# Buffer counts in a hybrid encoder layer: a second query buffer, a third raw weight buffer, and g_final in the output ring

## The chip, the cores and the metric

The kernel runs on one core of one Trainium2 chip. The metric is device time in microseconds (us) of one execution, given as the median of several runs. One execution was also taken by the hardware profiler; the rows of the profile come from that one.

## The reference

One step of one encoder layer over 2048 prompt tokens and 32 sample tokens, all in float32, width 1024:

```python
a = rmsnorm(h, g_attn)
qa, ka, va, qb, kb, vb = split_proj(a, w_in)       # one projection, 1024 -> 3072 columns
oa = diff_attn(qa, ka, va)   # 4 heads, two score maps of 64 dims each, 128-dim values:
                             # softmax(map 0) - lam * softmax(map 1), T5 bias, chunk-causal mask
ob = band_attn(qb, kb, vb)   # 8 heads of 64, each 64-token chunk sees itself and 8 before it
h = h + concat(rmsnorm(oa, subln_g) * (1 - lam_init), rmsnorm(ob, out_norm_b)) @ w_out
c = rmsnorm(h, g_mlp)
h = h + square(relu(c @ w_up)) @ w_down            # 1024 -> 4096 -> 1024
h = h + sigmoid(h @ w_ple_gate) * (p @ w_ple_proj)
y = rmsnorm(h, g_final)
```

The new keys and values are outputs too. The sample tokens also attend to a cache of 128 older positions.

## The kernel before, in words

Every float32 operand of a matmul is split into a high and a low part, and each product is made of three matmuls (`mm3`, lines 168 to 170): high by high, high by low, low by high. For a weight this is done by `wunit` (line 155): a DMA of 512 KB into a raw tile `wr` (two buffers), a copy to `wh` on ACT (line 149) and a subtraction to `wl` on POOL (line 153), three buffers each. Only after the subtraction is the raw buffer free for the next load. Every DMA of the kernel is issued by SyncE (line 144), whose queue works in order: a DMA that waits for its buffer holds up all behind it.

Tokens come in four blocks: three of 512, and a last one of 544 with the sample tokens. Half 0 is blocks 0 and 1, half 1 blocks 2 and 3. Written order: projection of half 0, first part of the differential attention (pairs of 128-query tiles 0 to 3, pool `a0`), the rest of the projections with the band attention, second part of the differential attention (pairs 4 to 7 and the sample tokens, pool `a1`), output projection and MLP of half 0 (one block after the other), gate and final norm of block 1, output projection of half 1, gate and final norm of block 0, MLP of half 1 (both blocks together), and the gates and final norms of blocks 2 and 3.

That is the order in which the program is written. The order in which each engine's queue runs is drawn up when the program is built, by a planner: it simulates the engines, prefers what is written earlier, and issues what is ready and has a buffer. So the second part of the attention runs in between the MLP of half 0. Within one ring of buffers, tiles are handed out in written order.

In the differential attention, `attn_a` goes over groups of pairs and, within a group, over 4 heads; for each head it loads the bias `ba` and the keys `ka` (one buffer each), and calls `attn_a_pair` for each pair. That one calls `load_q`, which issues four DMAs of 128 KB for the queries of the pair. The query tile `q` has two buffers in the first part (where `self.small` is true) and one in the second. For each of the pair's two query tiles follow the score matmuls (line 545), a maximum on DVE and the exponential on ACT (line 559), the combination of both maps (line 582); then for every four key tiles a load of values `v`, transposes (line 617) and the matmuls with the values (lines 631 to 633). The groups of the second part are `JA1 = [(4, 5), (6, 7, 8)]`, where 8 stands for the sample tokens: 8 loads of keys and 20 of queries.

The gate (`gate`) and the final norm (`final`) take their tiles from a ring: 8 slots (`uq`) for block 1, 16 slots (`up`) for the others; the same rings hold the MLP's hidden activations `uh` and `ul`. `final` transposes h back, takes the sum of squares and multiplies by 1/rms and by g_final (line 1054). g_final lies in a tile of its own, copied to all 128 partitions by `gfin` (line 962): once for block 1, and once more for the other three after the pools were changed.

Of the kernel before, what the change touches and what calls it, by code (L numbers as in the profile page):

```python
# [12 lines left out]
F32 = mybir.dt.float32  # L13
F32R = mybir.dt.float32r
# [5 lines left out]
P = 128  # L20
D = 1024
# [12 lines left out]
BLK = 544  # L34
# [10 lines left out]
def toks(b):  # L45
    out = []
    for i in range(4):
        out.append((i * P, P))
    if b == 3:
        out.append((512, SS))  # L50
    return out
# [81 lines left out]
class Kern:  # L133
# [20 lines left out]

    def wunit(self, src, shape, hi_eng="act", lo_eng="pool"):
        nc = self.nc
        raw = self.wp.tile([P] + shape, F32, tag="wr", bufs=2, name="wr")
        self.dma(raw, src)
        hi = self.wp.tile([P] + shape, F32R, tag="wh", bufs=3, name="wh")
        lo = self.wp.tile([P] + shape, F32R, tag="wl", bufs=3, name="wl")  # L160
        self.split(hi, lo, raw, hi_eng, lo_eng)
        return hi, lo
# [314 lines left out]

    def load_q(self, pool, gi, t0, n, maps):
        nc = self.nc
        q = pool.tile([P, len(maps), 2, 256], F32R, tag="q", bufs=2 if self.small else 1, name="q")  # L480
        for d in range(2):
            for i, m in enumerate(maps):
                self.dma(
                    q[64 * d : 64 * d + 64, i, :, :n],
                    self.qS[gi, :, 64 * m : 64 * m + 64, t0 : t0 + n].rearrange("l r c -> r l c"),
                )
        return q
# [471 lines left out]
            prev = us  # L959
        self.mlp_down(ch, nf, blocks, prev, st, wk, md)  # L960

    def gfin(self, pool):
        self.gf = pool.tile([P, D], F32, name="gf")
        self.dma(self.gf, self.a["g_final"].unsqueeze(0).broadcast_to([P, D]))

    def gate(self, b, h, up, act, md):
        nc, a = self.nc, self.a
        n, t0 = BN[b], 512 * b
# [48 lines left out]
    def final(self, b, h, up, fk, mm, md=None):  # L1017
        nc, a = self.nc, self.a
        t0 = 512 * b
        sts, yns = {}, {}  # L1020
        phased = md is not None

        def side(c0, tn, q):
            if phased:
                sts[c0] = st_all[:, c0 // P]
            elif q == 0:
                sts[c0] = fk.tile([P, 2], F32, tag="fst", bufs=6, name="fst")
            st = sts[c0]
            yp = (md if phased and q == 1 else mm).tile([P, 512], F32, tag="mm", name="yp")
            for k in range(4):  # L1030
                nc.tensor.transpose(yp[:tn, P * k : P * k + P], h[:, 4 * q + k, c0 : c0 + tn], self.ident)
            if phased and q == 1:
                yns[c0, q] = yp
            else:
                yns[c0, q] = up.tile([P, BLK], F32, tag="u", name="yn")[:, :512]
                nc.vector.tensor_copy(yns[c0, q][:tn], yp[:tn])
            junk = up.tile([P, BLK], F32, tag="u", name="junk")[:tn, :512]
            nc.scalar.activation(junk, yp[:tn], AF.Square, accum_out=st[:tn, q : q + 1])

        if phased:  # L1040
            st_all = fk.tile([P, 5, 2], F32, tag="fsa", name="fsa")
            nc.gpsimd.memset(st_all, 1.0)
            for c0, tn in toks(b):
                side(c0, tn, 0)
                yield
        def emit(c0, tn, r):
            tt = t0 + c0
            dst = a["y_prompt"][0, tt : tt + tn] if tt < SP else a["y_sample"][0, tt - SP : tt - SP + tn]
            for q in range(2):
                src = yn = yns[c0, q]  # L1050
                if phased and q == 1:
                    yn = up.tile([P, BLK], F32, tag="u", name="yo")[:, :512]
                g = self.gf[:tn, 512 * q : 512 * q + 512]
                nc.vector.scalar_tensor_tensor(yn[:tn], src[:tn], r, g, op0=ALU.mult, op1=ALU.mult)
                self.dma(dst[:, 512 * q : 512 * q + 512], yn[:tn])

        if phased:
            for c0, tn in toks(b):
                side(c0, tn, 1)
            ss = fk.tile([P, 5], F32, tag="fss", name="fss")  # L1060
            nc.vector.tensor_tensor(ss, st_all[:, :, 0], st_all[:, :, 1], op=ALU.add)
            r = self.rsqrt(fk, ss, 5, 1.0 / D, EPS, nc.vector, "rfa")
            for i, (c0, tn) in enumerate(toks(b)):
                emit(c0, tn, r[:tn, i : i + 1])
            return
        for c0, tn in toks(b):
            side(c0, tn, 0)
            side(c0, tn, 1)
            st = sts[c0]
            nc.vector.tensor_tensor(st[:tn, 0:1], st[:tn, 0:1], st[:tn, 1:2], op=ALU.add)  # L1070
            emit(c0, tn, self.rsqrt(fk, st[:tn, 0:1], 1, 1.0 / D, EPS, nc.vector, "rf", tn, 5))
            yield

    def run(self):
        tc, nc, a = self.tc, self.nc, self.a
        with ExitStack() as top:

            def opened(stack, name, bufs, space=None, side="left"):
                kw = {} if space is None else {"space": space}
                return stack.enter_context(  # L1080
                    tc.tile_pool(name=name, bufs=bufs, side=side, reuse_waits="tile", **kw)
                )
# [31 lines left out]
            with ExitStack() as x:  # L1114
                pool = opened(x, "a0", 1, side="right")
# [42 lines left out]
            with ExitStack() as x:  # L1158
                pool = opened(x, "a1", 1, side="right")
# [1 line left out]
                    self.attn_a(js, pool, ps_s, ps_t, ps_o)  # L1161
            wk = opened(sq_, "wk", 1)
            fk = opened(sq_, "fk", 1)
            self.gfin(fk)
            acc, cn, st = {}, {}, {}
            def norms(b, act, ps):
                self.colnorm(acc[b][0], b, 1.0 / D, wk, ps, "mm", self.rS)
# [10 lines left out]
            up = Sized(opened(top, "uh", 16, side="right"), BLK)  # L1178
# [24 lines left out]
            psx.close()  # L1203
            wk = opened(top, "wk4", 1)
            fk = opened(top, "fk4", 1)
            self.gfin(fk)
            md = opened(top, "md", 8 - MM, PSUM, "right")
            act = Sized(opened(top, "acth", 4), BLK, True)
            hh = opened(top, "hh", 2, side="right")
# [1 line left out]
            g = self.outproj(3, wk, oa[3], md, acc[3])  # L1211
# [4 lines left out]
            g = self.gate(0, h, up, act, md)  # L1216
# [12 lines left out]
            g = self.gate(3, st[3][0], up, act, md)  # L1229
# [54 lines left out]
```

## Time and profile before

| | us |
|---|---|
| median of 3 runs | 3329.38 |
| lowest and highest | 3328.49, 3332.86 |
| the profiled execution | 3334.02 |
| its span in the profile | 3332.1 |

How to read the profile: PE is TensorE's matmuls, PEld its weight loads, which overlap them, DVE is VectorE, POOL is GpSimd, SPq the queue of SyncE. A row of a group of instructions gives line, engine, operation, written tile and read tiles, the count, the busy time, and the idle time just before them with what ended it. A row of the waits gives who waited for whom, the total in us, how often, and the longest. A row in order of time gives the start, the duration, the instruction, and in brackets the idle time before it. A row of a stretch gives its bounds and length, the busy time and the count of instructions of PE, PEld, DVE, ACT and POOL, then PE's granted clock (1.00 is full), the busy share of the DMA engines and GB/s.

### The profile page before, as it was taken

What the parts mean: (1) busy time and instruction counts of PE and PEld (TensorE: products, weight loads), DVE (VectorE), ACT (ScalarE), POOL (GpSimd) and SP (SyncE); (2) the same over time, 40 slices, a digit from 0 to 9 for tenths busy, and PEclk for the clock granted to TensorE, in tenths of its full rate; (3) what the DMA queues carried; (4) which work ended last, traced back from release to release, by engine and by line L of the source; (5) the groups of instructions that cost most, each with busy time, mean ns of one, the idle gap of its engine ahead of it and who ended that gap; (6) DMA issues with size and microseconds to landing.
All of it is one profiled execution on the core that took longest, in us unless ns stands there. A gap on an engine that the chain in (4) does not pass through costs nothing.

```text
span 3332.1 us, 50114 instructions
## 1 busy us (share of the span) xinstructions
PE 3111.6 (93%) x17881; PEld 2723.4 (82%) x17881; DVE 1674.4 (50%) x3952; ACT 1705.5 (51%) x3717; POOL 1467.9 (44%) x1083
## 2 busy tenths in 40 slices
PE   6988989999999999989899999988989999999998
PEld 6877778889877888778787878877779999999987
DVE  5117777454555544566656665746542322223235
ACT  4226666566665666666666665654443223222245
POOL 4335654432324433534544443555753333333365
PEclk9998899999999999999999999999999999999999
DMA  7488777786788554544644454346631111111133
GB/s 227 160 253 235 214 212 202 213 241 205 209 238 234 159 139 126 143 137 133 197 134 123 129 136 130 121 135 222 181 114 51 45 45 45 45 47 49 45 91 102
DMA packets 519074, 488.93 MB, mean 147 GB/s; under 512 B 37885, under 2 KB 414017, under 8 KB 518825
## 3 DMA queue, kind: packets, MB, share of 16 engines
q1 hardware_dynamic: 518824, 485.73, 50.2%
q8 instruction: 142, 2.33, 0.3%
q14 instruction: 108, 0.88, 0.1%
HBM read 379.06 MB, written 110.49 MB: 147 GB/s over the span
## 4 chain that ended last, share of the span: by engine, by line
PE 71%; DMA 12%; DVE 7%; ACT 3%; issue 3%; POOL 2%; SPq 2%; DVEq 0%; POOLq 0%; ACTq 0%
PE dps L168 6%; PE dps L169 6%; PE dps L170 6%; PE ups L168 6%; PE ups L169 6%; PE ups L170 6%; PE s L545 3%; DMA q<-qS 3%; PE qps L168 3%; PE qps L169 3%; PE qps L170 3%; PE ob L744 2%; PE sb L704 2%; SPq L144 2%; DMA ka<-kS 2%
## 5 line engine op out<-in xcount | busy, mean ns | idle before, releaser
L153 POOL TENSOR_TENSOR wl<-wr,wh 128x1024 fp32r<-128x1024 f32 x338 | 819.8, 2427 | 1027.5 <-ACT wh L149 985.3
L949 DVE TENSOR_TENSOR h<-h,dps 128x512 f32<-128x512 f32 (+1 forms) x640 | 373.1, 585 | 590.9 <-PE dps L170 578.4
L149 ACT ACTIVATE wh<-wr 128x1024 fp32r<-128x1024 f32 x338 | 357.4, 1058 | 539.9 <-PE dps L169 294.8
L168 PE MATMUL dps<-uh,wh 128*128 128x512 f32 (+1 forms) x1280 | 460.6, 360 | 14.8 <-DVE h L949 11.1
L168 PE MATMUL ups<-cH,wh 128*128 128x512 f32 (+1 forms) x1280 | 452.5, 354 | 9.3 <-ACT relu L914 7.7
L170 PE MATMUL dps<-uh,wl 128*128 128x512 f32 (+1 forms) x1280 | 453.0, 355 | 0.0
L169 PE MATMUL dps<-ul,wh 128*128 128x512 f32 (+1 forms) x1280 | 453.0, 354 | 0.0
L170 PE MATMUL ups<-cH,wl 128*128 128x512 f32 (+1 forms) x1280 | 451.9, 353 | 0.0
L169 PE MATMUL ups<-cL,wh 128*128 128x512 f32 (+1 forms) x1280 | 451.9, 353 | 0.0
L168 PEld LDWEIGHTS dps<-uh,wh 128*128 128x128 f32 x1280 | 243.8, 190 | 49.8 <-DVE h L949 16.9
L168 PEld LDWEIGHTS ups<-cH,wh 128*128 128x128 f32 x1280 | 242.2, 189 | 41.3 <-ACT relu L914 7.9
L170 PEld LDWEIGHTS dps<-uh,wl 128*128 128x128 f32 x1280 | 242.9, 190 | 33.4
L169 PEld LDWEIGHTS ups<-cL,wh 128*128 128x128 f32 x1280 | 242.7, 190 | 31.1
L153 POOL TENSOR_TENSOR ul<-relu,uh 128x272 fp32r<-128x272 f32 (+1 forms) x160 | 176.0, 1100 | 206.3 <-ACT uh L149 203.6
L170 PEld LDWEIGHTS ups<-cH,wl 128*128 128x128 f32 x1280 | 242.3, 189 | 30.1
L169 PEld LDWEIGHTS dps<-ul,wh 128*128 128x128 f32 x1280 | 243.2, 190 | 27.0
L545 PE MATMUL s<-ka,q 128*128 128x256 f32 (+4 forms) x784 | 197.2, 357 | 50.4 <-DMA q<-qS 29.1
L168 PE MATMUL qps<-aH,wh 128*128 128x512 f32 (+1 forms) x640 | 230.2, 360 | 6.6 <-ACT wh L149 2.2
L169 PE MATMUL qps<-aL,wh 128*128 128x512 f32 (+1 forms) x640 | 228.3, 357 | 0.0
L170 PE MATMUL qps<-aH,wl 128*128 128x512 f32 (+1 forms) x640 | 227.9, 356 | 0.0
L559 ACT ACTIVATE e<-s,nm 128x512 f32<-128x512 f32 (+3 forms) x256 | 155.2, 611 | 102.7 <-DVE nm L551 65.2
L545 PEld LDWEIGHTS s<-ka,q 128*128 128x128 f32 (+1 forms) x784 | 137.4, 200 | 78.5 <-issue 27.3
(217 smaller groups left out, 7076.9 us busy)
## 6 DMA issues: line engine op xcount, KB each, us to landing
wr<-w_up SPq DMA_DIRECT2D x96, 512.0 KB, 4.2
wr<-w_down SPq DMA_DIRECT2D x96, 512.0 KB, 3.7
wr<-w_in SPq DMA_DIRECT2D x74, 512.0 KB, 4.9
q<-qS SPq DMA_DIRECT2D x256, 128.0 KB, 4.7
v<-vSa SPq DMA_DIRECT2D x64, 512.0 KB, 3.8
ka<-kS SPq DMA_DIRECT2D x32, 512.0 KB, 7.2
wr<-w_out SPq DMA_DIRECT2D x32, 512.0 KB, 5.0
wr<-w_ple_gate SPq DMA_DIRECT2D x32, 512.0 KB, 4.4
```

The source lines that it names most:

```text
L144: self.nc.sync.dma_start(dst, src)
L149: nc.scalar.activation(hi, raw, AF.Copy)
L153: eng.tensor_tensor(lo, raw, hi.bitcast(F32), op=ALU.subtract)
L168: nc.tensor.matmul(ps, lh, rh, start=start and i == 0, stop=False)
L169: nc.tensor.matmul(ps, lh, rl, start=False, stop=False)
L170: nc.tensor.matmul(ps, ll, rh, start=False, stop=stop and i == n - 1)
L545: nc.tensor.matmul(s, q[:, m, hl, P * qi : P * qi + nr], kt[:, m, k0 : k0 + n], start=hl == 0, stop=hl == 1)
L559: nc.scalar.activation(dst, src, AF.Exp, bias=nmx, accum_out=z[:nr, m, bi : bi + 1])
L704: nc.tensor.matmul(s, q[:, 0, hl, P * qi : P * qi + nr], kt[:, c : c + w], start=hl == 0, stop=hl == 1)
L744: nc.tensor.matmul(o[:, qa:qb], vt, pt[:kn, i - kfirst, qa:qb], start=x == 0 and y == 0, stop=x == len(order) - 1 and y == 1,)
L949: nc.vector.tensor_tensor(hv, hv, ps, op=ALU.add)
```

## The change

The raw weight tile gets three buffers. The query tile gets two in both parts of the attention. `gfin` and its resident tile go; `final` loads g_final itself, as two tiles of 512 columns from the ring it is given, at its start, and keeps them to its end.

```diff
     def wunit(self, src, shape, hi_eng="act", lo_eng="pool"):
         nc = self.nc
-        raw = self.wp.tile([P] + shape, F32, tag="wr", bufs=2, name="wr")
+        raw = self.wp.tile([P] + shape, F32, tag="wr", bufs=3, name="wr")
...
     def load_q(self, pool, gi, t0, n, maps):
         nc = self.nc
-        q = pool.tile([P, len(maps), 2, 256], F32R, tag="q", bufs=2 if self.small else 1, name="q")
+        q = pool.tile([P, len(maps), 2, 256], F32R, tag="q", bufs=2, name="q")
...
-    def gfin(self, pool):
-        self.gf = pool.tile([P, D], F32, name="gf")
-        self.dma(self.gf, self.a["g_final"].unsqueeze(0).broadcast_to([P, D]))
-
...
         sts, yns = {}, {}
         phased = md is not None
+        gf = []
+        for q in range(2):
+            gf.append(up.tile([P, BLK], F32, tag="u", name="gf")[:, :512])
+            self.dma(gf[q], a["g_final"][512 * q : 512 * q + 512].unsqueeze(0).broadcast_to([P, 512]))
...
-                g = self.gf[:tn, 512 * q : 512 * q + 512]
+                g = gf[q][:tn]
...
             fk = opened(sq_, "fk", 1)
-            self.gfin(fk)
...
             fk = opened(top, "fk4", 1)
-            self.gfin(fk)
```

## The prediction

> **What bounds the kernel now.** I read the profile page first, then busy time by stage, then the waits of PE in each stage, then the instructions around single stalls in order of time.
>
> ```profile
> span 3332.1 us, 50114 instructions
> PE 3111.6 (93%) x17881; PEld 2723.4 (82%) x17881; DVE 1674.4 (50%) x3952; ACT 1705.5 (51%) x3717; POOL 1467.9 (44%) x1083
> L545 PE MATMUL s<-ka,q 128*128 128x256 f32 (+4 forms) x784 | 197.2, 357 | 50.4 <-DMA q<-qS 29.1
> ```
>
> PE is busy 93% of the span; no other engine passes half, PE's own weight loads apart. So the change pays only where PE stands still, or where its clock is lowered. The score matmuls of the differential attention (line 545) wait 50.4 us, most of it for the query load. Three stretches by stage:
>
> ```profile
> 1350.00:2210.00 860.00, 804.98 (x4017) 672.85 (x4017) 540.16 (x1132) 525.29 (x1205) 396.05 (x283) 0.97 0.49 137
> 2210.00:2500.00 290.00, 255.35 (x1344) 217.67 (x1343) 152.14 (x200) 133.84 (x250) 178.81 (x109) 0.94 0.55 174
> 2500.00:3200.00 700.00, 700.00 (x4330) 634.89 (x4329) 204.32 (x384) 199.47 (x338) 240.84 (x157) 1.00 0.16 48
> ```
>
> The first is the second part of the differential attention, run between the MLP of the first token half: PE is idle 860 − 805 = 55 us. The second is the passage to the second half (gate, output norm, output projection): 35 us idle. The third, the MLP of the second half, has no idle time and full clock; more buffers can give nothing there. The waits of PE in the first:
>
> ```profile
> PE s L545 <- DMA q<-qS: 27.3, 11, 4.1
> PE dps L168 <- DVE h L949: 11.1, 11, 2.0
> PE s L545 <- issue: 4.1, 1, 4.1
> ```
>
> Half of the 55 us are waits for queries. The 4.1 us under "issue" are one more such stall at a head's first pair, just after its four query DMAs, so I count 27.3 + 4.1 = 31.4 us.
>
> **Second query buffer.** With one buffer the load of the next pair starts when the last score matmul of this pair has read the old one. Inside a head this is the whole story (SyncE's issues, then PE, in order of time):
>
> ```profile
> 1476.60 2.54 SPq L144 DMA_DIRECT2D q<-qS  x4
> 1482.84 1.31 PE L545 MATMUL s<-ka,q 128*128 128x384 f32 x6 [2.16 <-DMA q<-qS]
> 1665.57 0.59 PE L545 MATMUL s<-ka,q 128*128 128x384 f32 x2 [1.21 <-DMA q<-qS]
> 1761.85 1.19 PE L545 MATMUL s<-ka,q 128*128 128x512 f32 x2 [2.96 <-DMA q<-qS]
> 1999.80 0.76 PE L545 MATMUL s<-ka,q 128*128 128x512 f32 x2 [3.62 <-DMA q<-qS]
> ```
>
> Four DMAs go out in 2.54 us, the queries are there some six microseconds after the buffer came free, and PE stood 2.16 us. These four stalls inside heads are 2.16 + 1.21 + 2.96 + 3.62 = 9.95 us. A second buffer lets the load go a whole pair earlier (20 pairs in 850 us, so some 40 us), and they go. The other 21.4 us are at a head's first pair:
>
> ```profile
> 1704.82 2.61 SPq L144 DMA_DIRECT2D ka<-kS  x4
> 1708.90 4.37 SPq L144 DMA_DIRECT2D q<-qS  x4
> 1720.93 1.22 PE L545 MATMUL s<-ka,q 128*128 128x512 f32 x2 [4.07 <-DMA q<-qS]
> ```
>
> Here the keys, which keep their one buffer, are loaded too, and the queries queue behind them. With two buffers the queries can go ahead of the keys; the keys are then late next. How much is left I take from the first part of the same attention, which has two query buffers, one key buffer and as many key loads already (4 heads x 2 groups of pairs). Its waits of PE on line 545, from 230 to 600 us:
>
> ```profile
> PE s L545 <- issue: 5.5, 2, 3.2
> PE s L545 <- DMA ka<-kS: 5.2, 3, 2.8
> PE s L545 <- DMA q<-qS: 1.8, 1, 1.8
> ```
>
> That is 12.5 us for 8 key loads. Its keys took 6.8 us from issue to landing in the median, those of the second part 7.5 us:
>
> ```profile
> DMA to landing us min/median/max: 3.6/6.8/8.2
> DMA to landing us min/median/max: 5.2/7.5/12.0
> ```
>
> So 12.5 x 7.5 / 6.8 = 13.8 us should remain, and 31.4 − 13.8 = **17.6 us** go. Bounds: 9.95 (only the stalls inside heads) to 31.4 us (all). I take the value of the first part because it is the same code with the same two buffers.
>
> **The clock after a stall.** The column before the last two is the granted clock:
>
> ```profile
> 1450.00:1460.00 10.00, 9.72 (x46) 8.30 (x47) 6.11 (x12) 2.69 (x7) 0.00 (x0) 0.83 0.36 120
> 1480.00:1490.00 10.00, 7.31 (x37) 5.80 (x37) 7.19 (x11) 5.44 (x12) 6.91 (x6) 1.00 0.32 87
> 1530.00:1540.00 10.00, 9.19 (x35) 7.69 (x36) 3.04 (x5) 1.73 (x3) 2.40 (x1) 0.70 0.27 93
> 1760.00:1770.00 10.00, 8.15 (x35) 6.83 (x36) 8.19 (x14) 5.56 (x11) 2.58 (x2) 0.83 0.27 74
> 2070.00:2080.00 10.00, 7.84 (x38) 6.88 (x39) 2.98 (x8) 2.51 (x5) 0.00 (x0) 0.83 0.87 241
> ```
>
> After the stall of 2.16 us (1482.84) the clock stayed full; after the one of 2.96 us (1761.85) ten microseconds ran at 0.83, a loss of 1.7 us. Of the query stalls six are followed by a window at 0.83 (the first and last are shown) and one by 0.70: 6 x 1.7 + 3.0 = 13.2 us. I let it fall with the stalls, 17.6 / 31.4 = 0.56 of it: **7.4 us**. Bounds: 3.4 (the two windows after stalls inside heads) to 13.2 us. [...]
>
> **Third raw weight buffer.** Every weight unit is a 512 KB load, a copy to high parts on ACT and a subtraction on POOL that frees the raw buffer. From 2210 to 2500 us PE waits for weights:
>
> ```profile
> PE gps L168 <- ACT wh L149: 7.4, 1, 7.4
> PE ops L168 <- ACT wh L149: 3.7, 2, 3.0
> PE ops L170 <- POOL wl L153: 1.2, 2, 0.9
> 2381.75 8.22 SPq L144 DMA_DIRECT2D tmp<-hS  x4
> 2390.57 0.38 SPq L144 DMA_DIRECT2D wr<-w_ple_gate  x1
> 2397.44 0.80 PE L168 MATMUL gps<-hH,wh 128*128 128x512 f32 x1 [7.44 <-ACT wh L149]
> 2390.00:2400.00 10.00, 2.56 (x6) 2.10 (x7) 10.00 (x11) 7.10 (x11) 7.39 (x5) 0.64 0.69 196
> 2400.00:2410.00 10.00, 10.00 (x37) 7.72 (x37) 7.98 (x5) 1.50 (x2) 8.53 (x5) 0.85 0.48 151
> ```
>
> The 7.44 us come from a weight load that stood on SyncE behind four loads waiting 8.22 us for their own buffers. One buffer more lets that weight go out one unit earlier, ahead of them; it would save 7.4 us and the clock behind it, 3.6 + 1.5 = 5.1 us. Whether it goes ahead depends on the order that the planner draws up, so I take half of 12.5: **6 us**. Bounds: 0 to 7.4 + 3.7 + 1.2 + 5.1 = 17.4 us; a loss is the last rival below. In the other stages nobody on PE waits long for weights.
>
> **g_final in the output ring.** Two resident loads of 512 KB go, and eight of 256 KB come, two in each of the four final norms, each pair holding two slots of the ring (8 slots in the first half, 16 in the second). The old load took 4.3 us, and in the final norm of block 1 DVE has 11.4 us from the first copy to the first product that needs it:
>
> ```profile
> DMA to landing us min/median/max: 4.1/4.3/4.5
> 2256.23 0.69 DVE L1036 COPY yn<-yp 128x512 f32<-128x512 f32 x1 [0.51 <-PE yp L1031]
> 2267.60 1.42 DVE L1054 SCALAR_TENSOR_TENSOR yn<-yn,rsy,gf 128x512 f32<-128x512 f32 x2
> ```
>
> So the load is hidden if its slot is free when the norm begins. If not, SyncE waits with weight loads queued behind it; uncovered, four norms would pay 4 x 4.3 = 17 us. Six slots still hold one and a half tokens of four tiles each, so I charge **1 us** and keep 0 to 17. A gain is excluded, since PE waits for no g_final now. The memory adds up: the 4 KB of the third raw buffer are those of the resident g_final, and the attention's pool grows by 4 KB into 5.8 KB that lay free below it in the kernel before, so no stage begins later for want of space.
>
> **Sum.** 17.6 + 7.4 + 6 − 1 = 30 us. The profiled execution took 3334.02 us (its span 3332.1), 4.6 us over the median of the runs; it would take 3304 us, and the median goes from 3329.4 to **3299 us**. Own range of this case, from the bounds of its terms taken with some of the cancellation one may expect: 3280 to 3312 us.
>
> **Rivals.** Each queue's order is fixed when the program is built, by a planner's simulated times, and changes everywhere when a buffer count does; that is why these carry weight.
>
> First, the keys take the queries' place in full: at a head's first pair PE stands as long as before, under another name. For it: the keys' 7.5 us landing and their single buffer; against it: the first part's 12.5 us. Then only 9.95 + 3.4 = 13.4 us are won: 3316 us.
>
> Second, the second buffer does not do what it says: the order leaves the query loads where they were, or attention, no longer waiting for queries, waits at once for its exponentials (the 11.1 us for DVE above become more). Nothing is won: 3329 us.
>
> Third, slower, by one mechanism: the weight load that may now be issued earlier stands on SyncE ahead of key loads, waiting for POOL to free the raw buffer, and the keys wait behind it.
>
> ```profile
> SPq L144 <- POOL wl L153: 275.7, 68, 10.0
> ```
>
> SyncE spent 275.7 us in 68 such waits between 1350 and 2210 us, 4.05 us each. One of them ahead of each of the 8 key loads, uncovered, is 32.4 us, with 1.7 us of clock each 46 us: 16 us more than the 30 won, 3345 us. It decides from 2.05 us a key load on ((30 − 13.6) / 8). Against it: the weight waits are there already, and the same number of loads frees the same number of buffers.
>
> **How the numbers follow.** Chances: the forecast 0.44, the keys 0.22, nothing 0.08, the weight load ahead of the keys 0.26; the last is high because every order changes and PE has 93% to lose and 7% to win. What a measurement of this kernel can tell from no change is about 0.2%, 6.7 us. Faster by more: 0.44 + 0.22 = 0.66; within: 0.08; slower: 0.26. The range, 3280 to 3348 us, reaches from the forecast's good end to just past the slow rival; about 0.07 lies below and 0.11 above.
>
> **What would show it.** Right: in the second part of the attention no wait of PE for q<-qS inside heads, query loads issued before the key loads of the next head, a remaining wait on ka of some 14 us in all, a granted clock of 0.98 or more there, and PE's idle time falling from 55 to below 40 us; no wait of PE or DVE for the g_final tiles. Wrong: as many stalls on line 545 under ka, new stalls of PE for wh or h in the MLP that fills the attention, SyncE waiting longer for POOL ahead of keys or values, or a new wait of SyncE on the ring at the first final norm.

## The result, and the profile after

The changed kernel takes 3315.91 us in the median of five runs (3313.27 to 3318.21), the kernel before 3329.38 in the runs beside them: ratio 0.9955, 95% interval 0.9942 to 0.9969, so 13.5 us less where 30 were forecast. That is the number of the first rival, 3316 us; how far its mechanism goes with the number is told below. The profiled execution took 3313.27 us. The top of its page, and the group of the score matmuls (busy us, mean ns of one | idle us ahead of them):

```profile
span 3311.5 us, 50115 instructions
PE 3103.8 (94%) x17881; PEld 2716.0 (82%) x17881; DVE 1673.1 (51%) x3952; ACT 1697.6 (51%) x3717; POOL 1465.0 (44%) x1083
L545 PE MATMUL s<-ka,q 128*128 128x256 f32 (+4 forms) x784 | 193.5, 353 | 44.2 <-DMA q<-qS 19.6
```

The score matmuls still wait 44.2 us, after 50.4. The same three stretches as in the prediction, each put where its stage now runs (length, PE busy, ..., and at the end clock, DMA share, GB/s):

```profile
1341.00:2201.00 860.00, 812.97 (x4078) 679.51 (x4078) 538.26 (x1136) 530.58 (x1221) 409.13 (x295) 0.98 0.50 138
2201.00:2491.00 290.00, 254.45 (x1371) 218.29 (x1370) 161.68 (x207) 127.22 (x240) 170.73 (x101) 0.94 0.56 174
2491.00:3180.00 689.00, 689.00 (x4250) 623.74 (x4249) 198.50 (x373) 196.53 (x333) 236.01 (x154) 1.00 0.16 48
```

In the second part of the attention PE is idle 860 − 813 = 47 us, not 55 as before and not under 40 as forecast; in the passage to the second half it is idle 36 us, not 35. The waits of PE from 1340 to 2200 us (us in total, times, longest):

```profile
PE s L545 <- DMA ka<-kS: 10.6, 4, 3.9
PE s L545 <- DMA q<-qS: 8.4, 2, 5.4
PE dps L168 <- DVE h L949: 7.2, 12, 1.5
PE s L545 <- issue: 5.2, 1, 5.2
```

Before, 27.3 us stood under q and 4.1 under issue. Now it is 10.6 + 8.4 + 5.2 = 24.2 us, and nearly half of that is called keys. None of it lies inside a head. At one of the heads' first pairs, SyncE's issues in order of time, then PE, then (count, KB, us from issue to landing) the fourth key load and the first query load behind the keys, which are issued at 2036.68 and 2038.63:

```profile
2033.45 1.24 SPq L144 DMA_DIRECT2D q<-qS  x2
2034.73 3.85 SPq L144 DMA_DIRECT2D ka<-kS  x6
2038.63 7.59 SPq L144 DMA_DIRECT2D q<-qS  x6
2049.32 1.19 PE L545 MATMUL s<-ka,q 128*128 128x512 f32 x2 [5.22 <-issue]
ka<-kS SPq DMA_DIRECT2D x1, 512.0 KB, 9.0
q<-qS SPq DMA_DIRECT2D x1, 128.0 KB, 10.6
```

The queries have their second buffer, and yet they go out in one burst with the keys, some 15 us ahead of the first score: the buffer comes free only when the last pair but one of the head before is done, and in the group of three pairs the last one is the short one with the sample tokens. The first score reads the first and the third of the pair's four query loads, and the third is behind the keys: it lands at 2038.63 + 10.6 = 2049.2 us, after the keys, and just ahead of the score. So the 5.22 us called issue are a wait for queries, and so are the 5.39 us two heads earlier, at 1814.36, where the order of the loads is the same. At the four heads that follow a head of the group (4, 5), the first pair's load runs 40 us and more ahead of the keys; there PE waits for the keys, or not at all.

### The profile page after: what moved, and what is told of

Same layout as the page of the kernel before. It is cut to its first block, busy times and chain, and to the rows that moved or that the text cites. A ratio compares the mean times of both kernels' runs of the same rounds, so it can differ in the third digit from the quotient of the medians.

```text
span 3311.5 us, 50115 instructions
## 1 busy us (share of the span) xinstructions
PE 3103.8 (94%) x17881; PEld 2716.0 (82%) x17881; DVE 1673.1 (51%) x3952; ACT 1697.6 (51%) x3717; POOL 1465.0 (44%) x1083
## 4 chain that ended last, share of the span: by engine, by line
PE 38%; DVE 5%; DMA 4%; ACT 2%; issue 1%; POOL 1%; SPq 1%; DVEq 0%; POOLq 0%; ACTq 0%
PE dps L168 5%; PE ups L168 5%; PE ups L169 5%; PE ups L170 5%; PE dps L169 5%; PE dps L170 5%; PE s L545 2%; PE gps L168 1%; PE gps L170 1%; PE gps L169 1%; DVE e L582 1%; DMA ka<-kS 1%; DMA hd<-xT 1%; SPq L144 1%; PE tpp L617 1%
## 5 line engine op out<-in xcount | busy, mean ns | idle before, releaser
L545 PE MATMUL s<-ka,q 128*128 128x256 f32 (+4 forms) x784 | 193.5, 353 | 44.2 <-DMA q<-qS 19.6
```

The source lines that it names most:

```text
L545: nc.tensor.matmul(s, q[:, m, hl, P * qi : P * qi + nr], kt[:, m, k0 : k0 + n], start=hl == 0, stop=hl == 1)
```

## The experiments

Ratios are taken from runs made side by side, in several sets; in these the kernel before took 3323.9 to 3329.4 us in the median, so medians of different sets compare no more closely than that, and the ratios count. "Stalls" are the idle times of PE ahead of score matmuls in the second part; "second part" is the time from 3 us ahead of its first score matmul to its last one. Both come from one profiled execution.

| kernel | us, median | ratio, 95% interval | stalls, us | second part, us |
|---|---|---|---|---|
| before | 3329.4 | 1 | 34.9 | 809.5 |
| full change | 3315.9 | 0.9955 (0.9942 to 0.9969) | 25.2 | 791.4 |
| e1: query buffer | 3306.5 | 0.9932 (0.9917 to 0.9948) | 21.6 | 788.9 |
| e13: the same, g_final's load in two | 3306.9 | 0.9951 (0.9935 to 0.9968) | 24.8 | 790.1 |
| e2: raw weight buffer | 3314.4 | 0.9959 (0.9947 to 0.9972) | 27.1 | 804.1 |
| e3: ring | 3330.0 | 1.0011 (0.9999 to 1.0023) | 41.3 | 812.8 |
| e8: g_final's load in two | 3328.9 | 1.0006 (0.9996 to 1.0016) | 36.6 | 814.6 |
| e4: query buffer, ring | 3320.1 | 0.9977 (0.9963 to 0.9990) | 27.4 | 798.9 |
| e9: query and weight buffer, no ring | 3309.4 | 0.9954 (0.9942 to 0.9967) | 26.9 | 792.4 |
| e14: e4 with three query buffers | 3325.9 | 1.0010 (0.9997 to 1.0023) | 22.5 | 799.6 |
| e7: before, 6 of 8 key loads left out | 3295.8 | 0.9907 (0.9888 to 0.9926) | 15.3 | 779.7 |
| e5: full change, the same left out | 3295.3 | 0.9913 (0.9899 to 0.9927) | 8.2 | 776.1 |
| e12: keys by columns | 3306.3 | 0.9932 (0.9913 to 0.9951) | 16.1 | 810.6 |
| e10: keys by columns, query buffer | 3294.5 | 0.9919 (0.9901 to 0.9937) | 15.1 | 775.2 |
| e15: keys by columns, e14 | 3297.9 | 0.9925 (0.9907 to 0.9944) | 12.8 | 772.8 |
| e6: keys by columns, full change | 3296.0 | 0.9901 (0.9882 to 0.9919) | 11.2 | 763.6 |
| e11: keys by columns, e9 | 3292.2 | 0.9891 (0.9871 to 0.9912) | 10.3 | 760.1 |

The last column needs care: the planner runs more or less of the MLP inside the second part. For before, full change, e12 and e6, in this order:

```profile
1364.30:2173.80 809.50, 757.51 (x3785) 633.02 (x3784) 524.05 (x1095) 501.47 (x1160) 374.11 (x268) 0.97 0.50 139
1359.70:2151.10 791.40, 747.10 (x3757) 625.47 (x3757) 515.03 (x1084) 494.14 (x1151) 367.95 (x265) 0.98 0.51 142
1353.30:2163.90 810.60, 764.12 (x3811) 637.09 (x3810) 532.16 (x1098) 500.22 (x1168) 376.60 (x270) 0.98 0.49 140
1358.70:2122.30 763.60, 731.35 (x3720) 612.45 (x3720) 509.10 (x1083) 491.10 (x1152) 361.27 (x261) 0.99 0.51 146
```

PE's idle time there is 52.0, 44.3, 46.5 and 32.3 us. A second measure, worked out from the same traces, is the time from the end of the last score matmul of a head to the start of the first one of the next, summed over the seven changes of head: 108 us before, 92 in the full change, 110 in e12, 56 in e6.

**The three parts, each alone.** e1 changes `bufs=2 if self.small else 1` to `bufs=2`, e2 `tag="wr", bufs=2` to `bufs=3`, e3 moves g_final only; e4 is the full change without the raw weight buffer.

> The second query buffer alone. Theory Q (the whole gain comes from the query stalls inside heads): about 3316 us, as the full change, with no wait of PE for queries inside heads. Theory W (the third raw buffer gives part): 3322 us or more. Theory P (any new plan of the queues moves the time by ten or so microseconds, and the buffers matter little): anywhere from 3315 to 3340 us, without relation to the stalls.

> The third raw weight buffer alone. Theory Q: 3329 us, within 4 us of the kernel before, with the 27 us of query stalls still there and the 7.4 us wait for a weight in the gate of block 0 still there. Theory W: 3322 us or less. Theory P: anywhere from 3315 to 3340 us.

> g_final in the output ring alone. Theory Q: 3329 us, within 4 us of the kernel before. Were the loads of g_final exposed at the start of the four final norms, up to 17 us more: 3346 us. Theory P: anywhere from 3315 to 3340 us.

> The full change without the third raw buffer. Theory Q: 3316 us, as the full change. Theory W: 3322 us or more. Theory P: anywhere from 3315 to 3340 us.

The query buffer alone gains 22 us, the raw weight buffer 14, the ring nothing that can be measured. That is 36 us; the full change gives 13.5. The prediction had 25 us for the query buffer with its clock and 6 for the raw weight buffer: measured alone they give somewhat more than that together, but they don't add. Of the expectations, that of Theory Q held for e3 and that of Theory W for e2; e1 came out below all of them, and e4 between those of Q and W, in the band of P. Waits of PE in the second part, e1 first, then e2:

```profile
PE s L545 <- DMA ka<-kS: 8.4, 3, 5.1
PE s L545 <- issue: 7.6, 2, 5.4
PE s L545 <- DMA q<-qS: 0.7, 2, 0.4
```

```profile
PE s L545 <- DMA q<-qS: 21.6, 10, 3.8
```

With the raw weight buffer alone the queries' waits shrink too, from 27.3 to 21.6 us, though nothing of their loads was changed. So the two buffers take in part from the same waits. Where most of e2's 14 us come from, its trace doesn't show: its profiled execution, 3322.8 us, was one of the slowest of the twelve.

**A new order alone, and the buffers without the ring.** e8 gives the planner another program with the same work; e13 does the same beside the query buffer. e9 has both buffers, and keeps g_final out of the ring (for block 1 it takes two tiles of the work pool).

```diff
-        self.dma(self.gf, self.a["g_final"].unsqueeze(0).broadcast_to([P, D]))
+        for q in range(2):
+            self.dma(self.gf[:, 512 * q : 512 * q + 512], ...)
```

> The kernel before, with each resident load of g_final issued as two DMAs of 256 KB in place of one of 512 KB; no buffer and no size changes. Theory P (a new plan of the queues by itself moves the time by ten microseconds): outside 3321 to 3335 us, or the waits of PE on line 545 differ by more than 8 us from the 35 of the kernel before. Rival (plans with the same buffers take the same time): 3328 us within 4 us, with the stalls as before.

> The kernel before with two query buffers in the second part, and with one load of the resident g_final split into two DMAs: no work is added or taken away, but the planner draws up another order from there on. Theory P (the order that the planner happens to draw up moves the time by as much as the parts of this change do): the time differs from that of the query buffer alone (3306, ratio 0.9932) by 5 us or more, ratio outside 0.9917 to 0.9948. Theory W (the buffer alone is worth 22 us in any order, and the third raw weight buffer takes part of that back): 3303 to 3309 us, ratio 0.9917 to 0.9948.

> Second query buffer and third raw buffer as in the full change, but g_final not in the ring: for block 1 it is loaded into two tiles of the work pool just before the final norm, for the other blocks it stays resident as before. Theory R (holding two slots of the ring is what costs the second query buffer part of its gain): 3292 to 3304 us, the sum of the two buffers measured alone. Theory P (the plan of that kernel is unlucky, the ring is not the cause): 3306 to 3320 us, with no relation to the ring.

e8 equals before: a new order alone doesn't move the time there. e13 doesn't decide between its two theories. Its median and its second part equal those of e1, as Theory W has it; but its ratio, 0.9951, lies outside the band of Theory W, and beside the full change's 0.9955. So the query buffer alone is worth 22 us by e1 and 16 by e13, and that it beats the full change isn't clear of noise; that the parts don't add is, with 16 + 14 us too. e9 repeats the full change (0.9954 against 0.9955) with the same stalls, so the gain falls short without the ring too. The ring isn't thereby cleared: beside the query buffer alone it goes with a loss (e4 against e1, 0.9977 against 0.9932), whose cause was not followed further.

**The keys left out.** In e5 and e7 the heads 1 to 3 of each group in the second part use the keys of head 0, so 6 of the 8 key loads are left out; e5 is the full change, e7 the kernel before with one query buffer.

> The full change, and in the second part of the attention heads 1 to 3 of each group read the keys of head 0, so 6 of the 8 key loads are left out. Theory K (with two query buffers the keys are what is late at the start of a head, in the full change as much as the queries were before): the 24 us of waits of PE on line 545 fall below 8 us, with 1.7 us of clock a stall the time falls by 20 to 32 us from that of the full change, to 3284 to 3296 us. Rival (the stalls at the starts of heads are set by the queries that go out in the same burst): they stay, 3310 us or more.

> The kernel before (one query buffer), with the same 6 key loads left out. Theory K: the four stalls inside heads stay, some 10 us, and at the starts of heads the queries alone are late, as inside heads, 2.5 us for each of 6: 25 us of waits for queries, 3305 to 3318 us, and at least 15 us more than the full change without those key loads. Rival (the second query buffer is worth nothing once the keys are there): the same time as the other within 6 us.

Both take 3295 to 3296 us. Without the key loads the full change is worth nothing that four executions each can show. So most of its gain comes out of waits that the key loads make, the queries' own waits among them: PE's waits for queries in e7, with one buffer, are

```profile
PE s L549 <- DMA q<-qS: 9.3, 7, 4.5
```

(line 549 is 545 moved by the edit), where the kernel before has 27.3 + 4.1 us. The expectation for e7 said that the query waits would stay, some 25 us; it missed. That for e5 held.

**A third query buffer.** e14 is e4 with `bufs=2 if self.small else 3`.

> The changed kernel with two raw weight buffers as before, and with three query buffers in the second part, so that the first pair of a head can be loaded two pairs ahead, not in the same burst as the keys. Nothing is left out. Theory Q (what the second buffer leaves at the heads is that the queries still go out together with the keys): the query waits at the heads' first pairs fall to under 2 us, and the time goes 6 to 12 us below the run with two query buffers and the ring, to 3306 to 3314 us, ratio 0.993 to 0.996. Theory K (the keys alone hold the heads' first pairs): the key waits take the place, 17 us or more stay, and the time is within 5 us of that run, 3315 to 3325 us, ratio 0.996 to 0.999.

```profile
PE s L545 <- DMA ka<-kS: 13.0, 7, 4.9
PE s L545 <- DMA q<-qS: 0.3, 1, 0.3
1913.98 2.53 SPq L144 DMA_DIRECT2D q<-qS  x4
1917.20 3.85 SPq L144 DMA_DIRECT2D ka<-kS  x6
1929.72 1.22 PE L545 MATMUL s<-ka,q 128*128 128x512 f32 x2 [4.87 <-DMA ka<-kS]
```

The queries go out ahead of the keys, nobody waits for them (0.3 us), and PE stands 4.87 us for the keys at a head's first pair. Every wait for a load there is now one for the keys, 13.0 us, though less than the 17 that Theory K expected. The time isn't better than with two buffers, 3325.9 against 3320.1 us, and the ratio is worse (1.0010 against 0.9977). Why it is worse the traces don't show: the second part, 799.6 against 798.9 us, and the profiled executions, 3321.1 against 3320.6, are equal.

**The order of the key loads.** In the second group the keys of a head come in six loads: three stretches of columns for each half of the partitions, one half after the other (in the first group in four). The first score block reads columns 0 to 511 of both halves, so it waited for loads of 512 KB of which the second half's went out fourth. The edit goes by columns first, and cuts the first 1024 columns in two, so there are eight loads; order and size are changed together. It stands in e12 (before), e10 (query buffer), e15 (e14), e6 (full change) and e11 (e9):

```diff
-            for hl in range(2):
-                src = ...
-                for c0 in range(0, nk, 1024):
-                    c1 = min(c0 + 1024, nk)
+            cuts = [0, 1024] if self.small else [0, 512, 1024]
+            cuts = [c for c in cuts if c < nk] + ([2048] if nk > 2048 else []) + [nk]
+            for c0, c1 in zip(cuts, cuts[1:]):
+                for hl in range(2):
+                    src = ...
                     self.dma(kt[64 * hl : 64 * hl + 64, :, c0:c1], src[:, :, c0:c1])
```

> The kernel before with two query buffers in the second part, and with the key loads of a head put in another order: first the columns 0 to 511 of both halves, then 512 to 1023, then the rest, so that the first score block of a head waits for two loads and not for six. Nothing is left out. Theory K (with two query buffers it is the keys that come last at a head's first pair, 8.4 us in three waits in the run of the query buffer alone): the waits for keys fall to 3 us or less, and with the clock the time goes 5 to 10 us below that run, to 3297 to 3302 us, ratio 0.990 to 0.992. Rival Q (the queries are issued behind the keys and land last whatever the order of the keys): key waits become query waits, the sum at the heads' first pairs stays at 15 to 18 us, and the time stays at 3303 to 3310 us, ratio 0.992 to 0.9945.

> The same with three query buffers in the second part, and the key loads of a head in order of columns as well. Nothing is left out. If queries and keys each hold a part of the heads' first pairs, the sum of the waits there falls to 8 us or less, and the time to 3295 to 3306 us, ratio 0.990 to 0.993, near the run in which six of the eight key loads were left out (3295). If a third thing takes the place (the exponential on ACT, SyncE's own issue), 12 us or more of stalls stay at the score matmuls and the time is over 3308 us.

> The changed kernel with the key loads of a head in order of columns. Nothing is left out. Theory K (what the full change lost, it lost at the keys of the heads): the second part shrinks from 791 to under 776 us, the time to 3288 to 3296 us, ratio 0.988 to 0.991. Rival W (it was lost to the weights or the ring, outside the heads): the second part shrinks by 10 us or less and the time stays over 3300 us, ratio over 0.992.

> The kernel before with two query buffers, three raw weight buffers, g_final resident as tiles outside the ring, and the key loads in order of columns. Nothing is left out. Theory K: with the keys out of the way the raw weight buffer's 6 to 8 us behind the second part add to the run with the query buffer and the ordered keys (3294.5): 3286 to 3290 us, ratio 0.988 to 0.9895. Rival S (the buffers' gains overlap whatever the keys do): 3292 to 3300 us, ratio 0.990 to 0.993.

> The kernel before with nothing changed but the order of the key loads, by columns. Nothing is left out. Theory Q (with one query buffer the queries end last at the heads: 27.3 of the 31.4 us of these waits): the stalls at the score matmuls stay at 30 us or more and the time within 5 us of before, ratio 0.9985 to 1.0015. Theory K (the keys hold the heads in both kernels, and the queries only show because they are issued behind them): the stalls fall by 10 us or more, and the time by 10 to 20 us, ratio 0.994 to 0.997.

Waits of PE on score matmuls for loads in the second part of e12, then of e6:

```profile
PE s L546 <- DMA q<-qS: 11.9, 6, 4.7
```

```profile
PE s L546 <- issue: 5.9, 2, 4.0
PE s L546 <- DMA q<-qS: 2.7, 2, 1.8
PE s L546 <- DMA ka<-kS: 1.5, 1, 1.5
```

In the full change the edit works as expected: the second part shrinks from 791.4 to 763.6 us, of which 12 us are PE's idle time, 10 the clock's cost and the rest matmuls that run elsewhere, and the ratio falls from 0.9955 to 0.9901, some 18 us. From head to head the sum falls from 92 to 56 us, and with the query buffer alone (e1 to e10) from 85 to 56. So what the full change left at the heads, it left in good part at the keys. The last change of head, in e12 (three rows) and e6:

```profile
2048.58 0.31 PE L546 MATMUL s<-ka,q 128*32 128x160 f32 x2
2054.37 2.66 SPq L144 DMA_DIRECT2D q<-qS  x4
2063.98 0.88 PE L546 MATMUL s<-ka,q 128*128 128x512 f32 x3
2006.55 0.31 PE L546 MATMUL s<-ka,q 128*32 128x160 f32 x2
2014.51 0.39 PE L546 MATMUL s<-ka,q 128*128 128x512 f32 x1
```

e12, with one query buffer, is not so plain. The queries' waits fall from 27.3 + 4.1 to 11.9 us and the time by 23 us, more than Theory K expected, and Theory Q's numbers are missed. But in its trace the queries, issued behind the keys, still come last: from the last score of a head to the first of the next it takes as long as before (15.4 us in the rows, 110 us in all against 108), the second part is no shorter, and PE's idle time in it falls by 5.5 us only. In these stretches PE runs more of its other matmuls (452 against 409), and it waits elsewhere instead: 16.9 us for DVE's `h`, 11.1 before. In the rows the third query load, issued at 2055.8, takes 7.9 us and lands at 2063.7, just ahead of the score. So with one query buffer the queries do hold the heads, and where most of the 23 us come from is open. e10 came out 2.5 us below its band, with its ratio inside and its key waits at 3.8 us, not 3; e15 is inside.

The pair of buffers without the ring, keys by columns (e11), has the lowest median, 3292.2 us, but its interval overlaps those of e10 and e6. Whether the raw weight buffer adds anything to e10 is therefore open: e11's expectations were 0.988 to 0.9895 and 0.990 to 0.993, and 0.9891 with its interval fits both.

## Why the prediction was wrong, point by point

- **Stalls inside heads: right.** The four, 9.95 us, are gone; none is left in the full change.
- **Stalls at heads' first pairs: the step that failed.** "12.5 x 7.5 / 6.8 = 13.8 us should remain" was the term: 24.2 us remained, against 21.4 at these places before. "With two buffers the queries can go ahead of the keys" held at five of the eight heads; there the keys come last, 10.6 us. At the three others the loads that the first score needs still go out behind the keys, in whole or in part, and the queries come last, 2.98 + 5.39 + 5.22 = 13.6 us. So the first rival, the keys in the queries' place, is right for somewhat less than half of what remained, and its 3316 us were met partly by luck: it counted nothing for the weights, and stalls and clock together gave 7.2 + 3.5 = 10.7 us, not 13.4. Scaling from the first part of the attention was the fault. The prediction's "as many key loads already" counts heads: there a head's keys are two loads, 16 in all, and in the second part four or six, 40 in all. And its 12.5 us were one execution of one order: in the full change the same first part, with its loads unchanged, has 16.2 us under the same three names:

```profile
PE s L545 <- DMA q<-qS: 11.3, 3, 5.0
PE s L545 <- issue: 4.1, 2, 2.1
PE s L545 <- DMA ka<-kS: 0.8, 1, 0.8
```

  And the row that spoke against it was quoted: the keys go out just ahead of the queries, so with queries early, loads of keys that start only at the head's end come last; e14 shows this. Alone (e1) the query buffer leaves 8.4 + 7.6 + 0.7 = 16.7 us, near the 13.8.
- **The clock: the mechanism right, the size that of the first rival.** Summed over short windows across the second part, the clock granted cost 20.5 us before, 17.0 after, 13.6 in e1 and 6.8 in e6: 3.5 us gained, not 7.4. Windows behind four of the remaining stalls, of 2.98, 3.90, 5.39 and 1.42 us:

```profile
1360.00:1370.00 10.00, 7.32 (x27) 6.01 (x28) 4.38 (x8) 3.42 (x9) 2.34 (x1) 0.83 1.11 288
1430.00:1440.00 10.00, 6.10 (x19) 4.72 (x18) 9.62 (x19) 3.62 (x7) 3.66 (x3) 0.73 1.08 248
1814.00:1824.00 10.00, 9.64 (x40) 8.44 (x41) 2.07 (x3) 2.14 (x3) 2.09 (x1) 0.69 0.81 203
1928.00:1938.00 10.00, 9.61 (x52) 8.10 (x53) 1.42 (x3) 3.27 (x6) 2.06 (x3) 1.00 1.12 253
```

  After 3.90 and 5.39 us the ten microseconds ran at 0.73 and 0.69, after 1.42 us at full clock. But they ran at 0.83 after 2.98 us, as after the 2.96 us of the kernel before, and there also after a wait for DVE of 1.30 us (at 1593.95; 1590 to 1600 us ran at 0.83), while 2.16 us in the kernel before cost nothing (1480 to 1490 us ran at 1.00). So the length of a stall alone doesn't tell here what it costs. The term also priced only the stalls for queries, 13.2 of the 20.5 us.
- **The raw weight buffer: the wrong wait.** The 7.44 us stall in the gate was to go. It is 9.70 us now (9.7 in e2 and e9 too, and 7.4 in e1, with two raw buffers), because the gate's weight load again stands on SyncE behind four loads that wait for buffers of their own:

```profile
2357.59 8.19 SPq L144 DMA_DIRECT2D tmp<-hS  x4
2366.36 0.38 SPq L144 DMA_DIRECT2D wr<-w_ple_gate  x1
2373.24 0.79 PE L168 MATMUL gps<-hH,wh 128*128 128x512 f32 x1 [9.70 <-ACT wh L149]
```

  That the gain "depends on the order that the planner draws up" was said, and half of it was counted; none came there. The buffer alone still gives 14 us (e2), at the queries' waits (27.3 to 21.6 us) and at places that weren't found.
- **The sum: terms that share a wait were added.** Both buffers take from the stalls at the heads, which fall from 34.9 us to 21.6 by the one, to 27.1 by the other, and to 25.2 by both. With e13's 24.8 us the stalls don't tell the one from both; the time from head to head does: 84 to 85 us with two query and two raw buffers (e1, e13, e4), 92 to 93 with three raw ones (e9 and the full change). Why the order drawn up for three raw buffers is the worse one at the heads wasn't shown. With the keys by columns it isn't (56 us in e10, e6 and e11).
- **g_final in the ring: right as far as its loads go.** Nobody on PE or DVE waits for it. The loads take 4.7 us in the median; the first product that needs one runs 21.6 us after the first load's issue at 2216.81:

```profile
gf<-g_final SPq DMA_DIRECT2D x8, 256.0 KB, 4.7
2238.39 0.75 DVE L1054 SCALAR_TENSOR_TENSOR yn<-yn,rsy,gf 128x512 f32<-128x512 f32 x1
```

  Alone it costs 0.1% (e3), an interval that reaches to nothing. The loss of e4 against e1 stays without a cause.
- **The slow rival: not seen.** SyncE's waits for the subtraction on POOL from 1341 to 2201 us are as long as the 275.7 us before, and of the eight bursts of keys only the one at 1601.82 us goes out straight behind a weight load, which had waited 2.5 us for POOL:

```profile
SPq L144 <- POOL wl L153: 278.3, 63, 10.3
```

## What to carry to other kernels

When a wait for one load is taken away, another load of the same burst can come last in its place (e14: 0.3 us of waits for queries, 13.0 us for keys): before giving the waiting tile a buffer, ask what will come last once it is early, and price that from the very place, not from a like stage elsewhere. Where the last one is a big load, let its first pieces be small, and those that the first instruction reads: that gave some 18 us on top of the full change. With no buffer at all it gave 23 us, as much as the query buffer, though there the trace doesn't show how. The second query buffer took away the stalls inside heads (9.95 us gone) and not those at the heads (24.2 us in the full change, 21.4 before), where a third one gave nothing (e14 3325.9 us, e4 3320.1). Savings that shorten the same waits must not be added up: the two buffers gave 22 and 14 us alone, and 13.5 us in the full change, which has both. And a stall that shrinks is a gain only if the stage gets shorter: other work can fill it while the load lands as late as before (e12: 110 us from head to head, 108 before).

## What the hardware showed unexpectedly

In these traces the time to landing went with the company that a load had more than with its size. From 1350 to 2120 us in the full change, loads of equal size, one weight at a time against six key loads in a burst, and the smallest pieces of the keys, which go out in the same bursts (count, KB each, median us from issue to landing). The last row is the first key load of the burst shown above, at 2034.73; the fourth, of the same size and shape, took 9.0 us:

```profile
wr<-w_down SPq DMA_DIRECT2D x46, 512.0 KB, 3.9
ka<-kS SPq DMA_DIRECT2D x24, 512.0 KB, 8.0
ka<-kS SPq DMA_DIRECT2D x8, 80.0 KB, 8.7
ka<-kS SPq DMA_DIRECT2D x1, 512.0 KB, 5.4
```

A key load goes to 64 partitions and a weight load to 128, so between the first two rows the shape differs as well; inside the burst it doesn't.

And executions of one program spread by more than the change is worth: e2's twelve ran from 3306.26 to 3323.38 us, e4's from 3306.51 to 3330.57. A few microseconds between two single profiles, in stages whose work is the same, say nothing.
